# Where the split x lies in SBUF, counted from the weight tiles modulo 512 bytes: a float32 trunk of twelve blocks on one core

## The chip, the cores and the metric

The kernel is one program on one core of a Trainium2 chip. The metric is the time of one execution on the device, in microseconds (us). Before the change it is 2090.61 us, the median of 3 runs that lie between 2089.94 and 2092.35 us.

## The reference, cut to what matters

A trunk of four layers over 256 tokens of width 1024, all in float32. Each layer is a feed-forward block, a mixer and a second feed-forward block, so there are twelve blocks:

```
x = x + 0.5 * swiglu(rmsnorm(x, g1), w_gu, w_down)      # 1024 -> 2 * 2816 -> 1024
x = x + mixer(rmsnorm(x, g2))     # gated DeltaNet, stick-breaking attention, sparse attention, gated DeltaNet
x = x + 0.5 * swiglu(rmsnorm(x, g3), w_gu, w_down)
```

A last norm follows. Nearly all of the arithmetic is products of activations with float32 weights that are used once.

## The kernel before, in words

Everything is kept transposed, with features on the 128 partitions and tokens along the free axis. A float32 operand is split exactly into a high part (rounded to float32r) and a low part, and a product is the sum of three: hi\*hi, lo\*hi and hi\*lo, accumulated in PSUM. In a product `mm(out, w, x)` the 128 columns of `w` are loaded into the array (the profile calls this PEld), and `x` streams past as the moving operand (PE). All products are issued on L43.

**Weights.** A chunk of 128 x 2048 weights is fetched by one DMA into the tile `r`; ScalarE makes the high parts `h` (L170) and VectorE the low parts `l` (L171), in pieces of 128 x 512. There are ten buffers of `h` and ten of `l`.

**The split x.** At the start of a block `norm_in` (L225) multiplies x by the norm's gain and splits it into the tile `x2` (named x in the profile's rows): for each of the 8 k tiles 256 high columns, then 256 low columns. There is one buffer for it, filled anew in each of the twelve blocks.

**A feed-forward block** has 11 steps. In a step two chunks (gate and up) are multiplied by `tile_wide` (L284): for each of 2 M tiles and 8 k tiles, a pair of products follows: `h` against the 512 columns of high and low x, then `l` against the 256 high columns. This is 32 pairs in a step and 352 in a block. The result goes through `act` (L340) into the tiles `ah` and `al`, and `rows` (L295) multiplies the chunk of the down projection with them: 16 times three products of 256 columns, which is 48 in a step and 528 in a block (`mm3`: h with ah, l with ah, h with al).

**The mixers** project x with `tiles2` (L274): three products of 256 columns each. There are 16 chunks of 48 products in each of the two gated DeltaNet blocks, 8 in stick-breaking attention, 3 in sparse attention. Stick-breaking attention's values are made the other way round, with x as the loaded weights and `h`, `l` of 512 columns as the moving operand. The sparse attention has further products with its latents `lath`, `latl`. A mixer ends with `out_proj` (L360), 4 chunks of 48 products with the heads' outputs `oh`, `ol`.

**Where the tiles lie.** SBUF tiles are laid out pool after pool along a partition. Of the built program, the start of a tile within a partition, modulo 512 bytes, is:

| tile | before | after |
|---|---|---|
| `h`, `l` (every buffer) | 352 | 352 |
| `x2` | 352 | 352 + the block's place |
| `oh`, `ol`, `lath`, `latl` and all other tiles of 8 KB | 352 | 288 |
| `ah`, `al` (every buffer) | 32 | 480 |
| `bah`, `bal` (the gates' weights, 16 columns a k tile) | 0 | 448 |
| `sh`, `sl` / `ntri` (inside stick-breaking attention) | 320 / 0 | 256 / 448 |

The k tiles of a weight piece are 128 float32 = 512 bytes apart and those of `x2` 2048 bytes, so all products of one kind in a block have the same distance (start of the moving operand minus start of the loaded weights, modulo 512 bytes). Two kinds are exceptions: the gates' weights `bah`, `bal` step by 64 bytes from k tile to k tile, and one projection of the sparse attention (L994) loads 96 columns at steps of 384 bytes.

Of the kernel before, what the change touches and what calls it, by code (L numbers as in the profile page):

```python
# [20 lines left out]
P = 128  # L21
T = 256          # tokens
D = 1024
KT = D // P      # k tiles of the model width
F = 2816
NS = F // 256    # steps of a feed-forward block, 256 hidden columns each
# [3 lines left out]
RS = 1024.0      # scale of the residuals kept in float16  # L30

# Everything is kept transposed: [feature on partitions, token].  A float32 matmul operand x is split
# exactly into hi = x rounded to float32r and lo = x - hi; hi*hi + lo*hi + hi*lo in PSUM carries float32.


class Bank:
    """One PSUM bank that several accumulation groups share."""
# [16 lines left out]
    def tr(self, out, x):  # L54
        """Transposes a [128, 128] float32 tile; the only kind of write to its part of the bank."""
        self.nc.tensor.transpose(out, x, self.k.ident)  # L56
        self.k.now += 0.11
# [8 lines left out]
class Trunk:  # L66
# [31 lines left out]
    def table(self, name):  # L98
        """A mixer's constants, side by side."""
        t = self.wk.tile([P, 1024], F32, name="tab", tag="tab", bufs=1)  # L100
        src = self.a[name]
        self.nc.sync.dma_start(t[:, :src.shape[1]], src)
        return t
# [13 lines left out]
    def bank(self, tag="A"):  # L117
        """A: small products and a feed-forward's sums; G: the big projections."""
        return Bank(self, self.ps.tile([P, 512], F32, name="bank" + tag, tag=tag))

    # ---- interleaving: side work (generators) advances between groups of the big products.  A generator
    # yields how long (us on TensorE's clock, as counted here) its next stage's operands are expected to take,
    # or a condition that its next stage waits for.
# [6 lines left out]
    def pump(self, n=None):  # L130
        """Run up to n ready stages; only the first few (width) generators are under way."""
        for _ in range(n or self.burst):
            g = min(self.side[:self.width], key=self.due, default=None)
            if g is None or self.due(g) > self.now:
                return
            self.step(g)
# [8 lines left out]
    def wait(self, done):  # L145
        """Run side work until done()."""
        while not done():
            g = min(self.side[:self.width], key=self.due)
            assert self.due(g) < math.inf
            self.now = max(self.now, self.due(g))  # L150
            self.step(g)
# [8 lines left out]
    def chunk(self, src, w=2048, pw=512, pool=(), parts=1):  # L160
        """A [128, w] chunk of weights as (hi, lo) pieces of pw columns; the pieces in pool are split by GpSimd."""
        r = self.raw.tile([P, 2048], F32, name="r", tag="r")
        for i in range(0, w, w // parts):
            self.nc.sync.dma_start(r[:, i:i + w // parts], src[:, i:i + w // parts])
        return [self.piece(r[:, i * pw:(i + 1) * pw], pw, i in pool) for i in range(w // pw)]
# [8 lines left out]
    def first_chunk(self, src, n):  # L174
        """The kernel's start: the first chunk and x arrive in parts and are split as they come."""
        nc = self.nc
        r = self.raw.tile([P, 2048], F32, name="r", tag="r")
        part = lambda i: r[:, i * 512:(i + 1) * 512]
        load = lambda i: nc.sync.dma_start(part(i), src[:, i * 512:(i + 1) * 512])
        xs = lambda i: nc.sync.dma_start(self.x[:, 2 * i:2 * i + 2], self.a["x"][:, 2 * i:2 * i + 2])  # L180
        load(0), xs(0), nc.sync.dma_start(self.gains, self.a["gains"])
        xs(1), load(1), xs(2), xs(3), load(2), load(3)
        xg, pieces = self.xg_tiles(), []
        for i in range(4):
            if i % 2 == 0:
                pieces.append(self.piece(part(i // 2)))
            for j in (2 * i, 2 * i + 1):
                self.norm_tile(xg, n, j)
        pieces += [self.piece(part(i)) for i in (2, 3)]
        return pieces, xg  # L190
# [12 lines left out]
    def rsqrt(self, a, n):  # L203
        """Newton's iteration for a ** -0.5 on a small tile."""
# [10 lines left out]
    def xg_tiles(self):  # L215
        self.x2 = self.big.tile([P, KT, 2 * T], F32R, name="x2", tag="xg", bufs=1)
        return [(self.x2[:, j, :T], self.x2[:, j, T:]) for j in range(KT)]

# [6 lines left out]
    def norm_in(self, n):  # L225
        """x times the gain, split; the tokens' factors come later (rstd)."""
        xg = self.xg_tiles()
        for j in (0, 2, 4, 6, 1, 3, 5, 7):
            self.norm_tile(xg, n, j)
        return xg  # L230

    def spread(self, cols):
        """[token, 1] columns (SBUF) -> a bank with each as a row on all partitions."""
# [5 lines left out]
    def rstd(self, st):  # L239
        """1 / rms(x) per token, into st: compact [token, 2] and as rows [128, T]."""  # L240
# [28 lines left out]
    # GDN's chunks of the input projection, (kind, head pair): keys 0, values 1, queries 2, gate 3  # L269
    gdn_order = ((0, 0), (0, 1), (0, 2), (3, 0), (0, 3), (3, 1), (2, 0), (1, 0), (1, 1), (1, 2), (1, 3),  # L270
                 (2, 1), (3, 2), (2, 2), (2, 3), (3, 3))
    korder = (0, 2, 4, 6, 1, 3, 5, 7)    # the order in which a block's last products finish x

    def tiles2(self, pieces, xg, order=None):  # L274
        """Two M tiles (8 k tiles each) of one chunk into one bank."""
# [8 lines left out]
    def tile_wide(self, pieces, m, order=None):  # L284
        """One M tile into a bank: the columns of hi * hi and those of hi * lo + lo * hi side by side."""
# [9 lines left out]
    def rows(self, acc, pieces, a2, last, done=None):  # L295
        """acc[d, t] += w[f, d] a[f, t] for the chunk's two k tiles."""
# [73 lines left out]
    def gdn(self, i, n):  # L370
# [17 lines left out]
        # b and a: [16, T]  # L388
# [4 lines left out]
        # pairs (head, chunk of tokens) are kept in the order of the projections: head pair, chunk, head of the pair  # L393
# [13 lines left out]
        def gates():  # L407
# [29 lines left out]
            # E[j, i] = exp(G_i - G_j) for i >= j, else 0; eGb: exp(G_i) of the second chunk as rows  # L437
# [13 lines left out]
        def conv2(b, kind, c, dst):  # L451
            """Convolution and silu of two projected heads: dst [128, 2, T]."""
# [3 lines left out]
            # chunks are stored k, v, q; the convolution's channels q, k, v  # L456
# [18 lines left out]
        def keys(c):  # L475
# [23 lines left out]
            # A = I + L (unit lower triangular), transposed, in two float16 parts  # L499
# [8 lines left out]
            # the inverse X of A in float16 by merging blocks; XT its transpose  # L508
# [26 lines left out]
            # float32: with R = I - A X, the inverse is X + X R + X R R (+ X R^3, below float32)  # L535
# [46 lines left out]
        def delta(c):  # L582
# [36 lines left out]
            # the queries' factor s = dk^-0.5 / |q| goes into the output's norm: s * rsqrt(s^2 ss/128 + eps)  # L619
# [53 lines left out]
    def sb(self, n):  # L673
# [31 lines left out]
        def attend(h, qk):  # L705
            # z^T: [keys, queries]; columns: key tile 0 x all queries, key tile 1 x queries of tile 1
# [38 lines left out]
    def rms_factor(self, sq, n, ones, out):  # L745
        """rsqrt(mean of squares + eps) per token from a squared tile, into out [token, 2]."""
# [11 lines left out]
    def dsa(self, n):  # L758
# [15 lines left out]
        # tiles of the input projection: cq 0..2, index key | rotary key 3, ckv 4..5; 6: the normed index key  # L774
# [25 lines left out]
        def weights():  # L800
            """A query's weights of the index heads, times the factor of its latent, which relu lets through."""
# [6 lines left out]
        def latents(c, b):  # L808
            """Evacuate a chunk of the input projection: factor of the token, squares, gain and split."""
# [21 lines left out]
        def index_keys():  # L831
            """kidx[:, e]: the rotated index key in the rows of a tile's head e, zeros in the other's; rotary keys into K."""
# [49 lines left out]
        def select():  # L882
            """The 64 largest of each row are struck out; what is struck out and causal is selected: neg 0, else -1e30."""
# [33 lines left out]
        def attend(h):  # L917
# [21 lines left out]
            for i in range(3):       # (key 0, query 0), (key 0, query 1), (key 1, query 1)  # L939
# [26 lines left out]
        # the index first, so that the selection runs beside the projections of queries, keys and values  # L966
# [61 lines left out]
    def final(self, out):  # L1028
        """The last norm, beside the last products: to be called with each tile of x as it is done."""
# [53 lines left out]
def cols(w):  # L1083
    """[1024, n * 256] -> [n, 128, 2048]: per chunk two M tiles of 8 k tiles."""
# [4 lines left out]
def rows(w):  # L1089
    """[n * 256, 1024] -> [n, 128, 2048]: per chunk two k tiles."""  # L1090
# [4 lines left out]
def pack_ffn(gu, down):  # L1095
    out = np.empty((gu.shape[0], NS, 3, 128, 2048), gu.dtype)
    for l in range(gu.shape[0]):
        # a chunk: gate tile, up tile
# [6 lines left out]
def feat(g):  # L1105
    """[n * 128] -> [128, n]"""
    return g.reshape(-1, 128).T


def pack(x, ffn1_norm, ffn1_w_gu, ffn1_w_down, mix_norm, ffn2_norm, ffn2_w_gu, ffn2_w_down,  # L1110
# [41 lines left out]
    # constants of the shapes  # L1152
# [10 lines left out]
    for v, s in enumerate((2, 4, 8, 16, 32, 64)):  # L1163
        c = np.arange(64)
        blk = c // s                      # block of 2s of the c-th first-half column
# [41 lines left out]
```

## Time and profile before

| | |
|---|---|
| runs | 2089.94, 2090.61, 2092.35 us |
| the profiled execution: span from the first to the last instruction | 2092.3 us, mean granted TensorE clock 0.993 |
| TensorE matmul / weight load | 97% / 90% of the span busy |
| VectorE / ScalarE / GpSimd | 79% / 63% / 8% |
| DMA | 353.62 MB, mean 169 GB/s |

The views list no time of the profiled execution outside its span; the span lies inside the interval of the three runs, 1.7 us above their median. Busy times of PE are those of products that overlap: a product is recorded from its start to its modelled end, and the next one starts before that. What a product costs is therefore read from start to start, or from a run of products that the chain of waits gives as one piece with its time and count.

### The profile page before, as it was taken

What the parts mean: (1) busy time and instruction counts of PE and PEld (TensorE: products, weight loads), DVE (VectorE), ACT (ScalarE), POOL (GpSimd) and SP (SyncE); (2) the same over time, 40 slices, a digit from 0 to 9 for tenths busy, and PEclk for the clock granted to TensorE, in tenths of its full rate; (3) what the DMA queues carried; (4) which work ended last, traced back from release to release, by engine and by line L of the source; (5) the groups of instructions that cost most, each with busy time, mean ns of one, the idle gap of its engine ahead of it and who ended that gap; (6) DMA issues with size and microseconds to landing.
All of it is one profiled execution on the core that took longest, in us unless ns stands there. A gap on an engine that the chain in (4) does not pass through costs nothing.

```text
span 2092.3 us, 38898 instructions
## 1 busy us (share of the span) xinstructions
PE 2037.1 (97%) x14762; PEld 1886.2 (90%) x14762; DVE 1646.0 (79%) x3456; ACT 1308.2 (63%) x2804; POOL 161.9 (8%) x145
## 2 busy tenths in 40 slices
PE   8999899999999999999999998999999998999998
PEld 7999899999999989999989997899989998999997
DVE  7778898877887776777787789877787788988776
ACT  6566776665665566655665664765665667766654
POOL 1001311100100010100010013100010013111000
PEclk9999999999999999999999999999999999999999
DMA  7555333555455554555555542455555553235552
GB/s 256 195 188 182 102 105 123 173 190 187 171 206 188 195 179 140 176 184 197 185 184 199 182 153 76 162 187 196 184 182 199 184 179 106 100 119 182 182 199 84
DMA packets 52603, 353.62 MB, mean 169 GB/s; under 512 B 6976, under 2 KB 7872, under 8 KB 10688
## 3 DMA queue, kind: packets, MB, share of 16 engines
q1 hardware_dynamic: 52128, 350.49, 48.4%
q8 instruction: 116, 1.90, 0.4%
q14 instruction: 71, 0.58, 0.1%
q10 hardware_dynamic: 288, 0.66, 0.1%
HBM read 350.07 MB, written 1.05 MB: 168 GB/s over the span
## 4 chain that ended last, share of the span: by engine, by line
PE 82%; DVE 12%; ACT 4%; issue 1%; POOL 0%; DMA 0%; SPq 0%; ACTq 0%; DVEq 0%; POOLq 0%
PE bankG L43 55%; PE bankA L43 25%; DVE l L171 5%; ACT x L222 1%; DVE kT L466 1%; PE bankA L56 1%; ACT h L170 1%; DVE x L223 1%; DVE rs_t L211 1%; DVE x L302 0%; DVE rs_y L212 0%; DVE rs_t L210 0%; ACT sq L244 0%; DVE vT L466 0%; DVE pc L455 0%
## 5 line engine op out<-in xcount | busy, mean ns | idle before, releaser
L43 PE MATMUL bankG<-x,h 128*128 128x512 f32 (+1 forms) x4192 | 1269.0, 361 | 12.0 <-DVE x L223 12.0
L171 DVE TENSOR_TENSOR l<-r,h 128x512 fp32r<-128x512 f32 x1328 | 936.7, 713 | 374.1 <-ACT h L170 370.9
L170 ACT ACTIVATE h<-r 128x512 fp32r<-128x512 f32 x1328 | 823.0, 627 | 595.5 <-PE bankG L43 337.4
L43 PE MATMUL bankG<-x,l 128*128 128x256 f32 x3504 | 989.2, 282 | 0.0
L43 PEld LDWEIGHTS bankG<-x,h 128*128 128x128 f32 x4192 | 751.3, 189 | 130.1 <-DVE x L223 14.9
L43 PEld LDWEIGHTS bankG<-x,l 128*128 128x128 f32 x3504 | 666.5, 190 | 0.1
L43 PE MATMUL bankA<-ah,l 128*128 128x256 f32 x1408 | 389.2, 276 | 0.0
L43 PE MATMUL bankA<-ah,h 128*128 128x256 f32 x1408 | 389.2, 276 | 0.0
L43 PE MATMUL bankA<-al,h 128*128 128x256 f32 x1408 | 389.1, 276 | 0.0
L43 PEld LDWEIGHTS bankA<-ah,h 128*128 128x128 f32 x1408 | 264.4, 188 | 3.3
L43 PEld LDWEIGHTS bankA<-al,h 128*128 128x128 f32 x1408 | 264.5, 188 | 0.0
L43 PEld LDWEIGHTS bankA<-ah,l 128*128 128x128 f32 x1408 | 264.4, 188 | 0.0
L330 DVE TENSOR_TENSOR e<-e,bankG 128x256 f32<-128x256 f32 x352 | 145.9, 414 | 4.6 <-ACT e L329 4.6
L329 ACT ACTIVATE e<-bankG 128x256 f32<-128x256 f32 x352 | 129.3, 367 | 11.5 <-PE bankG L43 11.5
L245 POOL TENSOR_TENSOR sq<-sq 128x512 f32<-128x512 f32 x12 | 15.5, 1294 | 1473.8 <-ACT sq L244 1473.8
L342 DVE TENSOR_TENSOR e<-e,rb 128x512 f32<-128x512 f32 x176 | 121.0, 691 | 5.3 <-ACT rb L259 0.2
L199 ACT ACTIVATE ah<-e 128x256 fp32r<-128x256 f32 x176 | 72.6, 417 | 21.4 <-DVE e L344 21.3
L343 ACT ACTIVATE e<-e 128x256 f32<-128x256 f32 x176 | 71.3, 405 | 7.2 <-DVE e L342 7.2
L43 PE MATMUL bankG<-oh,h 128*128 128x256 f32 x256 | 74.5, 291 | 0.0
L344 DVE TENSOR_TENSOR e<-e 128x256 f32<-128x256 f32 x176 | 73.8, 419 | 0.7 <-ACT e L343 0.7
L200 DVE TENSOR_TENSOR al<-e,ah 128x256 fp32r<-128x256 f32 x176 | 73.1, 419 | 0.5 <-ACT ah L199 0.5
L43 PE MATMUL bankG<-oh,l 128*128 128x256 f32 x256 | 72.5, 283 | 0.0
(290 smaller groups left out, 1704.7 us busy)
## 6 DMA issues: line engine op xcount, KB each, us to landing
r<-in_ffn SPq DMA_DIRECT2D x262, 1024.0 KB, 4.9
r<-in_gdn_in SPq DMA_DIRECT2D x32, 1024.0 KB, 4.9
r<-in_gdn_out SPq DMA_DIRECT2D x8, 1024.0 KB, 4.9
r<-in_sb_qk SPq DMA_DIRECT2D x8, 1024.0 KB, 4.9
r<-in_sb_v SPq DMA_DIRECT2D x4, 1024.0 KB, 4.9
r<-in_sb_out SPq DMA_DIRECT2D x4, 1024.0 KB, 4.9
r<-in_dsa_out SPq DMA_DIRECT2D x4, 1024.0 KB, 4.9
r<-in_dsa_in SPq DMA_DIRECT2D x3, 1024.0 KB, 4.8
```

Source lines behind the costliest of these rows:

```text
L43: self.nc.tensor.matmul(out, lhsT, rhs, start=self.fresh, stop=stop, skip_group_check=True)
L56: self.nc.tensor.transpose(out, x, self.k.ident)
L170: self.nc.scalar.activation(h[:, :pw], src, AF.Copy)
L171: (self.nc.gpsimd if pool else self.nc.vector).tensor_sub(l[:, :pw], src, h[:, :pw].bitcast(F32))
L199: self.nc.scalar.activation(dh, src, AF.Copy)
L200: self.nc.vector.tensor_sub(dl, src, dh.bitcast(F32))
L211: nc.vector.scalar_tensor_tensor(t, t, -0.5, a, op0=ALU.mult, op1=ALU.mult)
L329: nc.scalar.activation(e[:, m * T:(m + 1) * T], b.t[:, :T], AF.Copy)
L330: nc.vector.tensor_add(e[:, m * T:(m + 1) * T], e[:, m * T:(m + 1) * T], b.t[:, T:])
L342: nc.vector.tensor_mul(e2, e2, st["rb"][:, None, :].to_broadcast([P, 2, T]))
L343: nc.scalar.activation(e[:, :T], e[:, :T], AF.Silu)
L344: nc.vector.tensor_mul(e[:, T:], e[:, T:], e[:, :T])
```

## The change

`xg_tiles` allocates the tile 448 bytes (112 float32) longer and places the split x inside it at an offset that depends on the block: 0, 192, 64, 128, 192, 192, 256, 256, 320, 384, 128 and 448 bytes for the blocks in their order. The eight feed-forward blocks so have the distances 0, 64, 128, 192, 256, 320, 384 and 448; the mixers 192 (gated DeltaNet), 192 (stick-breaking), 256 (sparse) and 128 (gated DeltaNet). Everything that is allocated behind `x2` moves by 448 bytes: the distance of `oh`, `ol` and of the latents from the weight tiles goes from 0 to 448, that of `ah`, `al` from 192 to 128. The rest of the diff removes comments. No instruction is added, removed or moved: TensorE has the same 14,312 rows in the same order before and after, and so have the other engines.

```
+    place = (0, 192, 64, 128, 192, 192, 256, 256, 320, 384, 128, 448)
-    def xg_tiles(self):
-        self.x2 = self.big.tile([P, KT, 2 * T], F32R, name="x2", tag="xg", bufs=1)
+    def xg_tiles(self, n):
+        o = self.place[n] // 4
+        t = self.big.tile([P, KT * 2 * T + 112], F32R, name="x2", tag="xg", bufs=1)
+        self.x2 = t[:, o:o + KT * 2 * T].rearrange("p (j t) -> p j t", j=KT)
         return [(self.x2[:, j, :T], self.x2[:, j, T:]) for j in range(KT)]
...
     def norm_in(self, n):
-        xg = self.xg_tiles()
+        xg = self.xg_tiles(n)
```

| products (moving operand) | count | distance before | after |
|---|---|---|---|
| `x2`, feed-forward pairs | 8 x 352 | 0 | 0, 64, 128, 192, 256, 320, 384, 448 |
| `ah`, `al` | 8 x 528 | 192 | 128 |
| `x2`, gated DeltaNet | 2 x 768 | 0 | 192, 128 |
| `x2`, stick-breaking, queries and keys | 384 | 0 | 192 |
| `x2`, sparse | 144 | 0 | 256 |
| `oh`, `ol` | 4 x 192 | 0 | 448 |
| `lath`, `latl` with 128 columns loaded | 108 | 0 | 448 |

## Rows read from the trace of the kernel before

**Rows 1.** The page's part 1, busy time of the engines.
```profile
PE 2037.1 (97%) x14762; PEld 1886.2 (90%) x14762; DVE 1646.0 (79%) x3456; ACT 1308.2 (63%) x2804; POOL 161.9 (8%) x145
```

**Rows 2.** The page's part 4, the chain that ended last, by engine.
```profile
PE 82%; DVE 12%; ACT 4%; issue 1%; POOL 0%; DMA 0%; SPq 0%; ACTq 0%; DVEq 0%; POOLq 0%
```

**Rows 3.** The chain in a feed-forward block, by line, 381.5 to 565.4 us.
```profile
by line: PE bankG L43 60.6%; PE bankA L43 29.3%; DVE l L171 4.2%; ACT x L222 1.1%; DVE x L223 0.9%; DVE x L302 0.8%; ACT h L170 0.7%; ACT sq L244 0.6%; DVE e L330 0.5%; issue 0.5%; DVE rs_y L212 0.3%; PE bankA L56 0.2%; DVE rs_t L210 0.2%; 
```

**Rows 4.** Busy time by stretch, the same block: engines, clock, DMA share, GB/s.
```profile
381.50:565.40 183.90, 183.38 (x1239) 168.00 (x1239) 142.64 (x269) 113.77 (x233) 5.34 (x4) 1.00 0.55 189
```

**Rows 5.** The chain in order of time, 700 to 800 us: start, length, what.
```profile
706.11 5.45 PE bankA L43 x48
711.56 11.10 PE bankG L43 x64
```

**Rows 6.** The same view in two mixers: queries and keys (776 us), `oh` (1325 us).
```profile
802.05 4.31 PE bankG L43 x36
...
1325.86 15.49 PE bankG L43 x129
```

**Rows 7.** Groups of PE instructions by form: count, busy us, mean ns of one.
```profile
L43 PE MATMUL bankG<-x,h 128*128 128x512 f32 x2816 | 990.2, 394 | 11.7 <-DVE x L223 11.7
...
L43 PE MATMUL bankA<-ah,l 128*128 128x256 f32 x1408 | 389.2, 276 | 0.0
L43 PE MATMUL bankA<-ah,h 128*128 128x256 f32 x1408 | 389.2, 276 | 0.0
...
L43 PE MATMUL bankG<-oh,l 128*128 128x256 f32 x256 | 72.5, 283 | 0.0
...
L43 PE MATMUL bankA<-sl,ntri 128*128 128x384 f32 x8 | 2.7, 340 | 0.0
```

**Rows 8.** Timeline of PE, stick-breaking attention's values: start, length, instruction.
```profile
753.12 0.61 PE L43 MATMUL bankG<-h,x 128*128 128x512 f32 x2
...
754.48 0.61 PE L43 MATMUL bankG<-h,x 128*128 128x512 f32 x2
```

**Rows 9.** Timeline of PE at the start of a gate projection.
```profile
595.37 0.39 PE L43 MATMUL bankG<-x,h 128*128 128x512 f32 x1
595.60 0.28 PE L43 MATMUL bankG<-x,l 128*128 128x256 f32 x1
595.71 0.40 PE L43 MATMUL bankG<-x,h 128*128 128x512 f32 x1
```

**Rows 10.** Timeline of PE in the sparse attention's projection L994, 96 columns loaded.
```profile
1286.78 0.28 PE L43 MATMUL bankG<-latl,h 128*96 128x256 f32 x1
...
1288.67 0.28 PE L43 MATMUL bankG<-lath,h 128*128 128x256 f32 x1
```

**Rows 11.** Busy time by stretch, those products: the last three are clock, DMA, GB/s.
```profile
1286.78:1288.67 1.89, 1.89 (x19) 1.89 (x17) 1.86 (x8) 0.64 (x1) 0.00 (x0) 1.00 0.00 0
```

**Rows 12.** Timeline of PE, the gates' products, 16 columns loaded.
```profile
195.62 0.28 PE L43 MATMUL bankA<-x,bah 128*16 128x256 f32 x1
...
198.28 0.28 PE L43 MATMUL bankA<-x,bal 128*16 128x256 f32 x1
```

**Rows 13.** The chain in the first gated DeltaNet block, by line.
```profile
by line: PE bankG L43 33.0%; PE bankA L43 15.8%; DVE l L171 11.8%; DVE kT L466 5.3%; issue 4.1%; PE bankA L56 3.6%; DVE vT L466 1.8%; DVE rs_t L211 1.8%; DVE pc L455 1.7%; DVE qT L466 1.6%; DVE rs_t L210 1.3%; ACT h L170 1.2%; DVE rs_y L212
```

More of the change, by code (lines that the diff above doesn't have):

```diff
@@ L182, in first_chunk @@
         xs(1), load(1), xs(2), xs(3), load(2), load(3)
-        xg, pieces = self.xg_tiles(), []
+        xg, pieces = self.xg_tiles(n), []
         for i in range(4):
```

## The prediction

> **What bounds the kernel now.** I read the shares of the engines first, then the chain that ended last, then the chain piece by piece, and last single products. PE is busy for 97% of the span [rows 1], and 82% of the chain lies on it [rows 2]. In a feed-forward block PE's two banks make up 60.6% + 29.3% of the chain [rows 3]; VectorE is busy for 142.64 of 183.90 us there and the DMA engines for 0.55 of the time [rows 4], so neither binds if PE speeds up by a per cent. In order of time such a block is a row of pieces without a gap: 64 products in 11.10 us, then 48 in 5.45 us, and again [rows 5]. What one product takes, from start to start, is therefore what the block takes, and the question is whether that depends on where its operands lie.
>
> It does. The products with `ah`, `al` take 5.45 us / 48 = 113.5 ns each [rows 5]. Products of the same shape, three in the same order, take 4.31 us / 36 = 119.7 ns with `x2`, and 15.49 us / 129 = 120.1 ns with `oh` [rows 6]. The granted clock is 1.00 in the feed-forward block [rows 4]. The modelled lengths repeat the step: 276 ns with `ah`, 283 with `oh` [rows 7]. The products with `ah` and with `oh` stem from one loop, `rows` (L295); what differs is the distance from the weights, 192 bytes for `ah` and 0 for `oh` and `x2`. I call 113.5 ns the quick pace and 120.0 the slow one; the step between them is 6.5 ns.
>
> Weight loads fill 90% of the span beside the products' 97% [rows 1]: a load runs beside the product ahead of it, both read SBUF at the same time, and the step looks like a clash of these reads. The Trainium skill (TensorE: Matmul & The Clock Gate, "Step-by-step: what each phase is for") says that TensorE has two independent read ports, one for the moving operand and one for the weights, and that loading the next weights takes no read bandwidth from the running product. By that the change would be worth nothing; here the trace disagrees, with 113.5 against 120.1 ns.
>
> **Which distances are slow.** The change uses every multiple of 64, and before has only 0 and 192 in products of full size. Two odd places tell of others. The projection with 96 columns loaded steps through the distances 0, 128, 256 and 384; its last 16 products, at the full clock [rows 11], take (1288.67 - 1286.78) / 16 = 118.1 ns [rows 10]. So these four are slow, all or nearly. The gates' products load 16 columns at steps of 64 bytes, so that the start of the weights alternates between even and odd multiples of 64; from the first to the 24th product, one of another kind among them, it is 23 steps in 2.66 us, 115.7 ns [rows 12], about half way. Both fit one rule, which I take: what counts is the distance modulo 128, multiples of 128 are slow, and 64 more than those are quick. Against it stands `sl`: 384 columns of length 340 ns. With the same tail as `ah` (276 - 113.5 = 162.5) this is a pace of 177.5 ns, where 113.5 x 384/256 would give 170 [rows 7]; it looks slow although its distance (288 to the next weights) is no multiple of 128.
>
> **The pair of a feed-forward block.** It takes 11.10 us / 32 = 346.9 ns [rows 5]. A product of 512 moving columns at distance 0 takes (754.48 - 753.12) / 6 = 226.7 ns [rows 8], twice 113.5, as if nothing clashed; the rest of the pair, 346.9 - 226.7 = 120.2 ns, is a slow product of 256. At the start of a gate projection one pair takes 0.34 us, 0.23 + 0.11 [rows 9]: a wide product as always with a quick one behind it. So I let a quick distance save 6.5 ns a pair. The bounds for the wide product are 0 and another 6.5 ns (if its 226.7 holds a clash and the least is 220).
>
> **The sum.** Each term is count times 6.5 ns, times the share that is on the chain.
> - `ah`, `al` go from 192, quick, to 128, slow: three groups of 1408 [rows 7], 4224 x 6.5 = +27.5 us. All of it is on the chain. If 128 costs only what the 96-column products show (118.1 - 113.5 = 4.6 ns), it is +19.4; if nothing, 0.
> - Feed-forward pairs: 2816 wide products [rows 7], 352 a block. Four blocks come to 64, 192, 320 and 448, quick: 4 x 352 x 6.5 = -9.2 us (bounds -9.2 and -18.3 from the wide product). The blocks at 0, 128, 256 and 384 stay as they are.
> - `oh`, `ol`, now at 448: 768 x 6.5 = -5.0 us; the piece of 129 products without a gap shows that they are on the chain [rows 6].
> - Gated DeltaNet at 192: 768 x 6.5 = 5.0 us of PE time, but PE has only 33.0% + 15.8% of the chain there, and VectorE's work most of the rest [rows 13]. I take half, -2.5 us (bounds 0 and -5.0). The other one, at 128, stays.
> - Stick-breaking attention at 192: 384 x 6.5 = -2.5 us. Its 96 wide products: 0, or -0.6 with the bound above.
> - Sparse attention at 256 stays; its latents' 108 products save 0.7 us at the most, half of it hidden: -0.3.
> - All other tiles behind `x2` keep their distances among themselves. Those that are read against constants ahead of it (a few hundred small products) have no row for either case; with 6.5 ns each way on some 500 of them it is 3 us of PE time at the most, mostly beside VectorE's work, and I take 0.
>
> The splits, evacuations and DMAs have the same sizes and order, and cost nothing new. Together: +27.5 - 9.2 - 5.0 - 2.5 - 2.5 - 0.3 = +8.0 us. On the span of 2092.3 us, whose 1.7 us above the median are within the scatter of the runs, this is 0.4%; on the median it gives 2098.6 us.
>
> **The rivals.**
> - *The wide product gains too.* The feed-forward pairs then give -18.3: 2090.6 - 1.2 = 2089.4 us. For it: 226.7 is 13.4 above 512/256 of 106.7 (256 columns at 2.4 GHz), just as 120 is 13.3 above 106.7, so both could hold one clash. Against it: the pair of 0.34 us, whose wide product is no shorter.
> - *128 is only half as bad for `ah`*, at the 118.1 ns of the 96-column products: 2098.6 - 8.1 = 2090.5 us.
> - *Only distance 0 (or 0 and 256) is slow*: then `ah` loses nothing. With seven feed-forward blocks gaining (7 x 2.3), both gated DeltaNets (5.0), stick-breaking (2.5), `oh` (5.0) and the sparse block (0.5), it is -29 us: 2061.6; with 0 and 256 slow, six blocks, -26.5: 2064. Against it stand the 118.1 ns at mixed distances, of which only a quarter were 0. This is the case on the other side. Its mechanism is that a clash needs the same place within 512 bytes; it decides as soon as `ah` at 128 takes under 118.1 ns, for there the loss falls below the gains of 19.5 us.
> - *Only 192 is quick.* Then 64, 320 and 448 give nothing, and one feed-forward block, one gated DeltaNet and stick-breaking attention gain 2.3 + 2.5 + 2.5 against 27.5: 2110.8 us. The `sl` products speak for it.
> - *No dependence at all.* Then 113.5 against 120 has another cause, such as where in SBUF a tile lies as a whole, and the time stays 2090.6 us. The gates' products between the two paces, with one and the same `x2`, speak against it. This is also where the Trainium skill's rule of two read ports (above) leads.
>
> **How the numbers follow.** I give the forecast 0.38, the wide product's gain 0.17, the half loss 0.10, the two cases without a loss 0.17, only 192 quick 0.13, and no dependence 0.05. The forecast's own range is 2089 to 2103 us, from its bounds (wide products, gated DeltaNet, small products). The range for the time is 2056 to 2114 us: it takes in all of these cases, and leaves out wide products gaining together with a harmless 128 (2045) and a 128 that is worse than 0. Under 0.2% (4.2 us) a measurement of this kernel hardly tells a change from none. Slower by more: most of the forecast (0.31), only 192 (0.13) and a little of the others, 0.46. Within it: 0.30, from the wide product's gain, the half loss and no dependence. Faster: 0.24, the cases without a loss and the better part of the wide product's gain.
>
> **What would show it.** In the chain of waits after, the pieces of 48 products with `ah` should take 5.76 us in all eight feed-forward blocks (5.45 now). The pieces of 64 should take 11.10 us in the blocks at 0, 128, 256 and 384, and 10.89 in those at 64, 192, 320 and 448; 10.68 there would be the wide product's gain. `oh` should come to 113.5 ns a product. If the 48 stay at 5.45, the step that failed is the rule modulo 128, and the kernel is faster; if the pieces at 64, 320 or 448 stay at 11.10, it is the other half of that rule, and the kernel is slower than forecast. A time outside the range would mean a clash that these two paces do not bound.

## The result and the profile after

The changed kernel takes 2115.24 us (median of 4 runs, 2114.20 to 2117.61) against 2090.36 us (4 runs on the same chip): a ratio of 1.0119, with a 95% interval of 1.0105 to 1.0134. It is 24.9 us slower, where +8.0 was forecast, and lies just above the range. The profiled execution has a span of 2113.3 us.

The page's first line and the first of its part 4, to be held against [rows 1, 2]:

```profile
PE 2057.3 (97%) x14762; PEld 1899.9 (90%) x14762; DVE 1645.3 (78%) x3456; ACT 1306.2 (62%) x2804; POOL 161.4 (8%) x145
...
PE 84%; DVE 11%; ACT 3%; issue 1%; POOL 0%; DMA 0%; SPq 0%; DVEq 0%; ACTq 0%; POOLq 0%
```

PE's busy time grew by 20.2 us and that of its weight loads by 13.7; the other engines stand within 2.0 us of where they were. The page counts 14,762 matrix instructions of PE before and after; the 14,312 rows given with the change are not its count. The same feed-forward block as in [rows 4], by stretch (engines, clock, DMA share, GB/s), is 4.65 us longer at the same clock:

```profile
381.55:570.10 188.55, 188.02 (x1240) 171.54 (x1239) 143.12 (x270) 113.99 (x235) 5.34 (x4) 1.00 0.53 185
```

The chain in order of time (start, length, what) says which pieces grew. Here are steps of the blocks at 0 (90 us), 64 (461 us), 128 (632 us) and 192 (895 us), and between and behind them mixer pieces: gated DeltaNet at 192 (210 us) and at 128 (1743 us), queries and keys of stick-breaking attention at 192 (807 us), and `oh` at 448 (364 us). The pieces of 64 at 1101, 1416, 1621 and 1943 us are of the blocks at 256, 320, 384 and 448:

```profile
90.28 11.10 PE bankG L43 x64
101.38 5.69 PE bankA L43 x48
...
210.98 4.01 PE bankG L43 x35
...
364.26 4.78 PE bankG L43 x42
...
461.28 11.30 PE bankG L43 x64
...
632.67 11.24 PE bankG L43 x64
643.91 5.70 PE bankA L43 x48
...
807.99 4.10 PE bankG L43 x36
...
895.74 11.30 PE bankG L43 x64
...
1101.21 11.10 PE bankG L43 x64
...
1416.35 11.30 PE bankG L43 x64
...
1621.69 11.24 PE bankG L43 x64
...
1743.16 4.17 PE bankG L43 x35
...
1943.42 11.30 PE bankG L43 x64
```

Against [rows 5], 48 products with `ah` went from 5.45 to 5.69 us. The 64 products of a gate or up projection stay at 11.10 us at distance 0, and as a rule (a block's first steps differ) take 11.30 at 64, 11.24 at 128 and 11.30 at 192; the blocks at 256, 320, 384 and 448 repeat these four values. So nothing got quicker there, and six blocks got slower. `oh` is at 4.78 us / 42 = 113.8 ns, queries and keys at 4.10 / 36 = 113.9 ns, both as forecast. The gated DeltaNet at 192 reached 4.01 / 35 = 114.6 ns; before, the same piece stood in the chain with 119.4 ns:

```profile
210.10 4.18 PE bankG L43 x35
```

Count times difference: rows 88 x 0.24 = +21.1 us; pairs 44 x 0.20 + 22 x 0.14 = +11.9; `oh` 768 x (113.8 - 120.1) ns = -4.8; stick-breaking attention 384 x (113.9 - 119.7) ns = -2.2; gated DeltaNet at 192, 768 x (114.6 - 119.4) ns, taken at half as in the prediction, -1.9. That is +24.1 of the 24.9 us. The two profiled executions are 21.0 us apart, but the one after had already reached its first product with `ah` 1.8 us earlier; from there on they differ by 22.9 us, so the pieces account for the change within about 1 us.

### The profile page after: what moved, and what is told of

The parts are those of the page before. It is cut to its first block, busy times and chain, and to the rows that moved or that the text cites. A ratio compares the mean times of both kernels' runs of the same rounds, so it can differ in the third digit from the quotient of the medians.

```text
span 2113.3 us, 38898 instructions
## 1 busy us (share of the span) xinstructions
PE 2057.3 (97%) x14762; PEld 1899.9 (90%) x14762; DVE 1645.3 (78%) x3456; ACT 1306.2 (62%) x2804; POOL 161.4 (8%) x145
## 4 chain that ended last, share of the span: by engine, by line
PE 84%; DVE 11%; ACT 3%; issue 1%; POOL 0%; DMA 0%; SPq 0%; DVEq 0%; ACTq 0%; POOLq 0%
PE bankG L43 55%; PE bankA L43 27%; DVE l L171 4%; DVE kT L471 1%; ACT x L227 1%; PE bankA L56 1%; DVE x L228 1%; ACT h L170 1%; DVE rs_y L212 1%; DVE rs_t L211 0%; DVE rs_t L210 0%; DVE vT L471 0%; DVE pc L460 0%; DVE qT L471 0%; ACT sq L249 0%
## 5 line engine op out<-in xcount | busy, mean ns | idle before, releaser
L43 PE MATMUL bankA<-al,h 128*128 128x256 f32 x1408 | 396.6, 282 | 0.0
L43 PE MATMUL bankA<-ah,l 128*128 128x256 f32 x1408 | 396.3, 281 | 0.0
L43 PE MATMUL bankA<-ah,h 128*128 128x256 f32 x1408 | 396.1, 281 | 0.0
```

What stands on the lines that cost most here:

```text
L43: self.nc.tensor.matmul(out, lhsT, rhs, start=self.fresh, stop=stop, skip_group_check=True)
```

## Experiments

The theory after the result: rows, pairs and mixers each have their own dependence on the distance, the rule modulo 128 is wrong, and pairs are at their best at 0. The main rival: the pairs got slower because the rows between them did. In all kernels below no arithmetic is changed unless said; the numbers in `place` are bytes, one for each block, and `...` marks lines left out. Ratios are to the kernel before on the same chip, with the 95% interval.

**x at 0 everywhere, the longer tile kept.** Only the tiles behind `x2` stay moved.

```
-    place = (0, 192, 64, 128, 192, 192, 256, 256, 320, 384, 128, 448)
+    place = (0, 0, 0, 0, 0, 0, 0, 0, 0, 0, 0, 0)
```

> The changed kernel with all places at 0: x2 is back at distance 0, ah and al stay at 128, oh and ol at 448. Theory A (each kind of product has its own pace, set by its own distance, and the terms add): pieces of 64 gate and up products back at 11.10 us in all eight feed-forward blocks, pieces of 48 rows at 5.70, oh at 113.5 ns; the time is that of before + 21 (rows) - 5 (oh), about 2106 us. Rival B (a clash is carried from the rows into the gate and up products behind them): the pieces of 64 stay near 11.3 in blocks that are now at 0, and the time stays near 2113 us or above.

Measured: 2106.92 us (2105.71 to 2108.53), ratio 1.0075 (1.006 to 1.009). A step in the chain:

```profile
427.67 11.10 PE bankG L43 x64
438.76 5.69 PE bankA L43 x48
```

The pairs are back at 11.10 us although the rows between them stay at 5.69: for rows at 128 the rival is out. Rows and `oh` alone cost 2106.92 - 2091.49 = +15.4 us against the kernel before on the same chip (21.1 - 4.8 = 16.3). The places of `x2` themselves so cost 24.9 - 15.4 = 9.5 us net, where the prediction had -14.2 for pairs and mixers.

**Rows back at 192.** The places of the change stay, and a gap of 64 bytes ahead of `ah` restores its old distance.

```
+            if not self.gap:
+                self.gap = self.small("gap", [P, 16], bufs=1)
+                nc.gpsimd.memset(self.gap, 0.0)
             ah, al = self.w2("ah", F32R), self.w2("al", F32R, "wb")
```

> The changed kernel with 64 bytes more ahead of ah and al, which are so back at distance 192; x2 and oh as in the changed kernel. Theory A: pieces of 48 rows back at 5.45 us, pieces of 64 as in the changed kernel (11.30 at 64 and 192, 11.23 at 128, 11.10 at 0); the time is that of the changed kernel less 21 us, about 2094. Rival B: the pieces of 64 fall with the rows to 11.10 or less, and the time is 2080 to 2085 us.

Measured: 2101.07 us (2100.46 to 2103.28), ratio 1.005 (1.0033 to 1.0066). The expectation was some 2094 us; the 7 us above it are in the rows. Blocks at 64 (423 us) and 192 (887 us):

```profile
423.11 11.29 PE bankG L43 x64
434.39 5.45 PE bankA L43 x48
439.84 11.31 PE bankG L43 x64
451.15 5.65 PE bankA L43 x48
...
887.88 11.31 PE bankG L43 x64
899.19 5.65 PE bankA L43 x48
```

At one distance the rows have two paces, 5.45 and 5.65 us. Behind the pairs at 64 they alternate, behind those at 128 nearly all and behind those at 192 all are slow, behind those at 0 nearly all are quick. So their pace goes with the run ahead, which no step of the prediction had. The kernel before holds both paces too, the slow one in the first step of several blocks:

```profile
589.88 5.66 PE bankA L43 x48
595.53 11.29 PE bankG L43 x64
606.83 5.45 PE bankA L43 x48
```

**All distances of the pairs in steps of 32**, one for each feed-forward block, with rows at 192 and `oh` at 0 (one run).

```
+    place = (0, 64, 32, 64, 64, 96, 128, 0, 160, 192, 192, 224)
...
-        t = self.big.tile([P, KT * 2 * T + 112], F32R, name="x2", tag="xg", bufs=1)
+        t = self.big.tile([P, KT * 2 * T + 128], F32R, name="x2", tag="xg", bufs=1)
```

> The eight feed-forward blocks at distances 0, 32, 64, 96, 128, 160, 192 and 224, ah and al at 192 and oh at 0 as before, the first gated DeltaNet and stick-breaking attention at 64, the second gated DeltaNet at 192. Theory A with a period of 256 bytes: pieces of 64 take 11.10 us at 0, 11.30 at 64 and 192, 11.23 at 128, those at 32, 96, 160 and 224 lie between their neighbours; the pieces of 48 rows 5.45 throughout. Products of 256 columns at 64 in the mixers: 113.5 ns if 64 is as quick as 192, 120 if 192 alone is quick. Rival B: the pieces of 64 are at 11.10 in all blocks, as the rows between are quick.

Measured: 2104.82 us. The chain at 32 (426 us), 64 (595 us) and 96 (892 us), and queries and keys at 64 (803 us):

```profile
426.24 11.11 PE bankG L43 x64
...
595.60 11.31 PE bankG L43 x64
...
803.24 4.24 PE bankG L43 x36
...
892.17 11.21 PE bankG L43 x64
```

The rest: 128 11.22, 160 11.11, 192 11.31, 224 11.10 to 11.30 us. No distance beats 0. That 160 lies below both of its neighbours was not expected, nor were the rows, all at 192: 5.44 to 5.46 us behind the pairs at 0, 96, 160 and 224, 5.65 behind those at 32, 128 and 192, and both in turn behind those at 64. The narrow products of the mixer at 64 take 4.24 / 36 = 117.8 ns, not 113.5: an odd multiple of 64 is not quick as such, and the rule modulo 128 falls here by itself.

**All distances of the rows in steps of 32**, with `x2` at 0. `ah` and `al` get five buffers of 320 columns (six of 256 before), and a block's place in them (one run).

```
+    row_place = (0, 0, 64, 96, 0, 128, 160, 0, 192, 224, 0, 32)
...
+            o = self.row_place[n] // 4
-            ah, al = self.w2("ah", F32R), self.w2("al", F32R, "wb")
+            ah, al = (self.wk.tile([P, 320], F32R, name=v, tag=tag, bufs=5)[:, o:o + 256] for v, tag in (("ah", "wa"), ("al", "wb")))
```

> x2 and oh at distance 0 as before; ah and al at 192 in the first feed-forward block, then at 0, 32, 64, 96, 128, 160 and 224 (five buffers of each in place of six, each 256 bytes longer). Theory A: pieces of 48 rows take 5.45 us at 192, 5.76 at 0 and 5.70 at 128; at 64 they take 5.45 if multiples of 128 are slow and the odd multiples of 64 quick (the rule of the prediction), 5.70 if 192 alone is quick; the pieces of 64 stay at 11.10 in all blocks. Rival B: the pieces of 64 rise to 11.2 or 11.3 in the blocks whose rows are slow.

Measured: 2114.36 us. Rows at 0 (438 us) and at 32 (610 us), with the pairs behind them, all at 0:

```profile
438.65 5.75 PE bankA L43 x48
444.40 11.31 PE bankG L43 x64
...
610.56 5.65 PE bankA L43 x48
616.21 11.10 PE bankG L43 x64
```

The rest: 64 5.65, 96 5.76, 128 5.69, 160 5.64, 192 5.45, 224 5.68 us. Only 192 is quick. The pairs too have two paces at one distance: 11.31 behind rows at 0 (11.30 behind those at 64 and 224), 11.10 behind rows at 32. For other rows than those at 128 the rival therefore holds in part.

**Every product where it was seen to be quickest:** pairs at 0, mixers and rows at 192, `oh` at 448 (the gap as above).

```
+    place = (0, 192, 0, 0, 192, 0, 0, 192, 0, 0, 192, 0)
```

> x2 at distance 0 in the eight feed-forward blocks and at 192 in the four mixers, oh and ol at 448, ah and al at 192 (64 bytes more ahead of them). Theory: the wide pair is quickest at 0 and all other products at 192, and the rows at 192 keep the quick pace when the pairs ahead of them are at 0 (as before). Pieces of 64 at 11.10 us, of 48 at 5.45, oh and x2 in the mixers near 114 ns; the time is that of before - 8 to -10, 2081 to 2083. Rival (the pace of the rows hangs on where the tiles lie as a whole, not on the run ahead): some blocks have rows at 5.65, and the time is 2090 or more.

Measured: 2084.40 us (2083.09 to 2086.05, 5 runs), ratio 0.9965 (0.9954 to 0.9977); it beats both kernels and lies a little above the 2081 to 2083 us expected. A step is 11.10 + 5.45 us, as before; the gain is the mixers' and `oh`'s.

```profile
406.34 11.10 PE bankG L43 x64
417.44 5.45 PE bankA L43 x48
```

**The wide product as two of 256, everything at 192** (all twelve places 192, the gap ahead of `ah` as above). A narrow product at 192 is quick, so three of them should beat the pair.

```
-            b.mm(b.t, wh, self.x2[:, j], False)
-            b.mm(b.t[:, T:], wl, self.x2[:, j, :T], q == KT - 1)
+            b.mm(b.t[:, :T], wh, self.x2[:, j, :T], False)
+            b.mm(b.t[:, T:], wl, self.x2[:, j, :T], False)
+            b.mm(b.t[:, T:], wh, self.x2[:, j, T:], q == KT - 1)
```

> x2 at distance 192 in all twelve blocks, ah, al at 192 and oh, ol at 448, and the wide product of the gate and up projections made as two of 256 columns, so that every product of a feed-forward block has the same shape and distance (three weight loads for a k tile in place of two). Theory W (what made the pair slow at 192 is that wide and narrow products alternate; products of one shape at 192 have no clash): pieces of 96 products at 10.9 us where a piece of 64 took 11.10, rows at 5.45, time 2063 to 2068. Rival R (the tile x2 is slow at 192 whatever the shape): 96 products take 11.3 us or more and rows 5.65, time 2110 or more.

Measured: 2084.52 us, with 10 runs between 2073.89 and 2092.81; ratio 0.9963 (0.9947 to 0.998). The profiled execution had a span of 2073.7 us. Its chain in two blocks with the same places:

```profile
407.79 10.88 PE bankG L43 x96
418.67 5.44 PE bankA L43 x48
...
879.48 11.31 PE bankG L43 x96
890.79 5.65 PE bankA L43 x48
```

The same two blocks by stretch (the last three columns are clock, DMA share, GB/s):

```profile
402.35:549.20 146.85, 146.85 (x1298) 146.85 (x1298) 105.52 (x198) 88.94 (x181) 0.00 (x0) 1.00 0.54 194
873.83:1015.00 141.17, 141.17 (x1201) 141.17 (x1201) 97.96 (x184) 82.40 (x168) 0.00 (x0) 1.00 0.52 187
```

Both blocks execute the same products from places that are alike (modulo 512 bytes), and one of them holds 113.3 ns a product, the other 117.8, through all its steps. The granted clock is 1.00 in both and the DMA traffic about the same, so neither is what divides them. One block of the eight was slow in this execution; with 11 x (11.31 - 10.88 + 5.65 - 5.44) = 7.0 us a block, zero to three more slow ones would make the scatter of the runs. That the runs differ by this is argued, for only one was profiled. The expected 2063 to 2068 us were missed: the pieces of 96 came out as expected, and without its slow block the profiled execution (2075.43 us) would come to 2068.4.

**The split product at all distances:** the scan of the pairs with the split product; stick-breaking attention is at 128 (one run).

```
+    place = (0, 64, 32, 64, 128, 96, 128, 0, 160, 192, 192, 224)
```

> The wide product made as two of 256 columns; the eight feed-forward blocks at 0, 32, 64, 96, 128, 160, 192 and 224, ah and al at 192, oh at 0. Theory W: the pieces of 96 follow the rows' scan per product: about 11.5 us at 0 and 96, 11.3 at 32, 64, 128, 160 and 224, 10.9 at 192 (or 11.3 there, if the run is entered in the other state). Rival R: they follow the pairs' scan, 11.1 at 0, 32 and 160, 11.3 at 64 and 192.

Measured: 2117.12 us; pieces of 96 by distance: 0 11.50, 32 11.20, 64 11.31, 96 11.52, 128 11.39, 160 11.39, 192 10.88, 224 11.35 us. Apart from 32 and 160 it is the order of the rows' scan: narrow products, three in a group, are quick at 192 alone, from `x2` as from `ah`.

**`l` moved against `h`** by 64, 128 and 192 bytes (a gap tile ahead of its buffers), which gives the wide product (it runs beside the load of `l`) and the narrow one (beside the load of `h`) different distances; one run each. The lines shown are the first kernel's; the gap has 32 and 48 columns in the others, whose places are set to give the distances of the table below.

```
+        nc.gpsimd.memset(self.lop.tile([P, 16], F32, name="gap", tag="gap", bufs=1), 0.0)
+    place = (192, 192, 0, 64, 192, 128, 192, 192, 0, 64, 192, 128)
```

> The low weight tiles l start 64 bytes later than h modulo 512, so the wide product (which runs beside the load of l) and the narrow one (beside the load of h) have distances of their own. Feed-forward blocks: wide/narrow 192/0, 0/64, 64/128, 128/192, and the same four again; rows beside h at 192, beside l at 128. Theory (each load has its own cost by the distance of the product it runs beside): pieces of 64 are slow (11.3) wherever the product whose distance decides is at 64 or 192 - if the wide one decides, the first and third blocks of each four; if the narrow one, the second and fourth. Rival (only the run as a whole has a pace, its products share one phase): no such pattern, all four between 11.1 and 11.3 with changes inside a block, and rows near 5.65 in all.

> Every buffer of l starts 128 bytes later, counted modulo 256, than the buffers of h, so a product that runs ahead of a load of l has a distance 128 smaller than beside a load of h. The feed-forward pairs get the distances (wide product 512 columns / narrow product 256 columns) 128/0, 192/64, 0/128 and 64/192, each in two blocks. Theory Y (a pair goes by the place of both of its products together, and repeats for blocks with the same two distances): both blocks of a kind have the same piece of 64, and a kind of which one half was seen to be quick (wide at 0 with narrow at 64, 10.92 us) need not be quick here; between 10.9 and 11.3 us for all four. Theory Z (the distance of one of the two products decides): if the narrow one, 192/64 takes 10.92 us as 0/64 did; if the wide one, 0/128 takes 10.92 us. Rows at 192 beside h but 64 beside l: by both theories not 5.45 but about 5.66 us a piece of 48. One run near 2108 us, from eight blocks of 11.1 to 11.2 and 5.66.

> As the run with l 128 bytes on, but with l 192 bytes on: the pairs get (wide/narrow) 64/0, 128/64, 192/128 and 0/192, each in two blocks; rows lie at 192 beside h and at 0 beside l. Theory Y (both together): both blocks of a kind alike, each kind with a value of its own between 10.9 and 11.3 us. Theory Z: if the narrow product's distance decides, 128/64 takes 10.92 us as 0/64 did; if the wide one's, 0/192 does. Rows about 5.66 to 5.75 us a piece of 48 by both. One run near 2108 us.

Measured: 2108.11, 2094.61 and 2108.59 us. The first kernel's blocks with the distances 0/64 (409 us), 64/128 (594 us) and 128/192 (892 us), wide/narrow:

```profile
409.86 10.92 PE bankG L43 x64
...
594.57 11.11 PE bankG L43 x64
...
611.36 11.31 PE bankG L43 x64
...
892.48 11.30 PE bankG L43 x64
```

The second kernel's with 192/64 (408 us), 0/128 (592 us) and 64/192 (888 us):

```profile
408.24 11.09 PE bankG L43 x64
419.33 5.49 PE bankA L43 x48
...
592.55 11.26 PE bankG L43 x64
...
888.15 11.29 PE bankG L43 x64
```

All pieces of 64, in us, by both distances (a range where they differ from step to step):

| wide \ narrow | 0 | 64 | 128 | 192 |
|---|---|---|---|---|
| 0 | 11.10 | **10.92** | 11.26 | 11.20 |
| 64 | 11.20 | 11.31 | 11.09 to 11.31 | 11.29 |
| 128 | 11.10 | 11.10 | 11.24 | 11.20 to 11.30 |
| 192 | 11.10 | 11.09 | 11.09 | 11.31 |

Neither row nor column decides: with the narrow product at 64 there are 10.92, 11.31, 11.10 and 11.09. That one product's distance alone decides is out; what was expected of the two together held, and blocks with the same two distances agreed in each kernel. Within a column x and `h` lie at the same places modulo 256 and only `l` moves, so the place of x alone does not decide either. At 64/128 the pieces go round in turn through 11.11, 11.31, 11.09 and 11.09 us, with no change of place. The rows at 192 beside `h` and 64 beside `l` took 5.49 us where 5.66 was expected, a miss, and so the second kernel took 2094.61 us where some 2108 were.

**The quickest pair in all blocks,** 0/64: `l` of gate and up chunks 64 bytes on in buffers of 576 columns, of which nine fit where ten were; rows at 192 beside both.

```
-        self.lop = pool(name="lo", bufs=10)
+        self.lop = pool(name="lo", bufs=9)
-        l = self.lop.tile([P, 512], F32R, name="l", tag="l")
+        l = self.lop.tile([P, 576], F32R, name="l", tag="l")[:, on:on + 512]
...
+    place = (64, 192, 64, 64, 192, 64, 64, 192, 64, 64, 192, 64)
```

> The quickest pair seen so far (wide product at distance 0, narrow one at 64: 10.92 us a piece of 64) in all eight feed-forward blocks, with ah and al at 192 beside both h and l, and oh and the mixers at 192 modulo 256. The lower pieces of l in gate and up chunks lie 64 bytes on in buffers of 576 columns, nine of them where there were ten. Theory Y (the pace is a property of the run of products in order, pairs and rows each by their own distances, and of the run ahead): pieces of 64 at 10.92 us and rows at 5.45 us save 88 x 0.18 = 15.8 us against the kernel with the wide products at 0: about 2068 us; if the pairs at 64 put the rows behind them into the slower of their two paces (5.65), 88 x 0.2 = 17.6 us are lost again: about 2086 us. Theory Z (the narrow product at 64 is not what made the pair quick, but the rows ahead of it with their mixed distances): pieces of 64 at 11.1 or 11.3 us, 2084 to 2102 us. One l buffer less: nothing by both, for the chunks come well ahead of their use.

Measured: 2095.32 us (2092.99 to 2099.75, 12 runs), ratio 1.0023 (1.0014 to 1.0032).

```profile
730.43 10.92 PE bankG L43 x64
741.35 11.31 PE bankA L43 x96
```

The pairs take 10.92 us in all eight blocks, and the rows behind them fall into their slow pace (5.65 us a piece of 48; the last piece above holds two, 11.31). That would be 2086 us, as expected for this case; 9 more were lost elsewhere. The waits of PE for the split x (us in total, times, longest), here and then in the kernel with the pairs at 0:

```profile
PE bankG L43 <- DVE x L229: 18.3, 18, 6.2
```

```profile
PE bankG L43 <- DVE x L229: 12.0, 11, 6.3
```

**Nine buffers of `l` alone,** in the kernel with the pairs at 0; no distance changes.

```
-        self.lop = pool(name="lo", bufs=10)
+        self.lop = pool(name="lo", bufs=9)
```

> The kernel with the wide products at distance 0 and the rows at 192, but with nine buffers of l in place of ten; no distance changes. It is to say where the run with the pairs at 0 and 64 lost 9 us more than its pieces of 64 and 48 (10.92 and 5.65 us, both as expected) account for. Theory M (the ninth buffer: with one l buffer less VectorE, which makes l and at a block's end also the split of x, falls behind at the block boundaries, where PE waited 18.3 us in place of 12.0 for the split x): some 2092 to 2095 us against 2084.4, with steps of 11.10 + 5.45 us inside the blocks and longer waits for x at their starts. Theory N (the loss comes from the distances, at the products between the pieces): 2084 to 2085 us, no change.

Measured: 2097.28 us (2095.51 to 2099.22), 12.9 above the kernel with ten; its ratio to before is 1.003 (1.0018 to 1.0041).

```profile
PE bankG L43 <- DVE x L229: 19.5, 17, 7.7
```

So the missing buffer, which had been expected to cost nothing, accounts for the 9 us; why it costs some 4 us more here was not settled. Inside the blocks a step is still 11.10 + 5.45 us; the loss is at the blocks' starts and in the mixers, of which the longer wait for the split x is 7.5 us.

## Why the prediction was wrong

- **What binds was read rightly.** It is the pace of PE's products, and that does depend on where their operands lie; the cause that the prediction gave for it, a clash of reads, was not tested. The Trainium skill's rule of two independent ports (TensorE: Matmul & The Clock Gate, "Step-by-step: what each phase is for"), weighed ahead of the run, would have left the time alone; 113.5 against 119.8 ns for one kind of rows in the rows' scan, by their place alone, speaks against it.
- **The step that failed is the pair's term, -9.2 us, which measured +11.9.** The prediction split 346.9 ns into a wide product of 226.7 that no clash touches and a slow narrow one, and let the narrow one become quick at 64, 192, 320 and 448. The pieces show no gain at any of the places used: 353 ns a pair at 64 and 192, 351 at 128. The table says why such a split can't be made: the pair's pace goes by both distances together. What carried the split was one pair of 0.34 us read off hundredths [rows 9]. It opens the very gate projection that was slow in the kernel before, 11.29 us / 32 = 352.8 ns a pair (595 us, shown with the second experiment). This step alone is 21.1 us, more than the whole miss of 16.9.
- **The rule behind it, quick at odd multiples of 64, was wrong as well.** Of the distances tried, with `h` and `l` alike, narrow products are quick at 192 alone, counted modulo 256 (`oh` at 448 is as quick as 192). Two odd places, 96 and 16 columns loaded, had carried the rule; both mix several distances, which fix no period. The row that spoke against it, `sl` [rows 7], was set aside.
- **The rows' term had the right sign and was mis-sized:** +21.1 for +27.5 us. 128 is less slow than 0 (5.69 against 5.75 us a piece), near the prediction's lower value of 118.1 ns: 5.69 / 48 = 118.5.
- **`oh` (-5.0; -4.8) and stick-breaking attention (-2.5; -2.2) were right,** since both came to 192 modulo 256 from 0. The gated DeltaNet at 128 kept its pace (4.17 us for 35 products), as forecast. Its twin at 192 came to 114.6 ns. How much of that the block's end saw no run isolates: from the last product with `ah` of the first block to the first of the next the kernel after is 2.1 us shorter than before and the kernel with x at 0 1.1 us, so some 1 us by estimate, where -2.5 was forecast; but the same two kernels differ by 1.1 us the other way at the second gated DeltaNet.
- **Of the rivals, "only 192 is quick" (2110.8 us) came nearest.** It was right on the narrow products at 64 and 128, but gave nothing to 448, where `oh` was quick, and it missed by the pairs at 64, 128 and 192, which it left as they were or made quicker.
- **Not foreseen: two paces at one distance.** Rows at 192 take 5.45 or 5.65 us, in two kernels by the pairs ahead of them, and the pairs at 0 11.10 or 11.31. The change itself hardly shows it, for its rows at 128 stay near 5.69. The kernel before had shown it: in the first step of several blocks its rows took 5.66 and its pairs 11.29 us, in the later steps 5.45 and 11.10 [rows 5].

Open is why these distances: no run looked at the reads themselves, so a clash between the moving operand and the next weights is an explanation that fits, not one that was shown. Nor was a shift of all operands together tried, nor found what puts a block into one pace or the other.

## What to carry to other kernels

Where TensorE is the bound and its pieces have no gaps, the place of the moving operand against the weights is worth up to 6% of a narrow product's time (113.3 to 120.0 ns), so measure it: give each repeated block its own distance in one run, and read the pieces. Don't transfer the value from one kind of product to another, or from a mixture of places to a rule; a sequence of products has to be scanned as it stands, with the sequence ahead of it. And count what the padding displaces: one buffer less cost 12.9 us here, more than the best placement of the same products gained (7.6).

## What the runs showed of the hardware

- Products of 256 float32r columns took 113.3 to 120.0 ns (10.88 us / 96; 5.76 us / 48), by their places and the run that they stand in; the granted clock was 1.00 in the blocks of both (402 to 549 us of the split product at 192, 1083 to 1225 us of the rows' scan).
- The pattern repeats after 256 bytes: blocks at 0 and 256, 64 and 320, 128 and 384, 192 and 448 have the same pieces (11.10, 11.30, 11.24 and 11.30 us).
- The quickest pair, 10.92 us / 32 = 341.3 ns, is within about 1 ns of the sum of the quickest wide product and the quickest narrow one (226.7 [rows 8] + 113.5 [rows 5] = 340.2).
- The same products from places that are alike run at one of two paces through a whole block (10.88 or 11.31 us for 96), in one and the same execution.
